# Where the tokens of a feed-forward layer are normalised: in place behind the third pair of products, instead of all at the seventh pair

## The chip, the core and the metric

The kernel runs on one core of a Trainium2 chip. A core has engines that work side by side, each through its own queue of instructions in order: TensorE (PE in the profile, with its weight loads as PEld) for matrix products, VectorE (DVE), ScalarE (ACT) and GpSimd (POOL) for work element by element, and SyncE (SP), which here only issues transfers. Products land in PSUM, eight banks of 128 x 512 floats; everything else lies in SBUF. The metric is the time of one execution on the device in microseconds (us), median over runs.

## The reference

Two layers of an encoder over 512 tokens of width 1024, all in float32. Each layer is an attention block of two kinds of heads, a cross-attention over 256 memory tokens, and a feed-forward block; then a last norm. The change lies in the feed-forward block:

```python
def rms_norm(x, g):
    x32 = x.astype(jnp.float32)
    y = x32 * lax.rsqrt(jnp.mean(x32 * x32, axis=-1, keepdims=True) + EPS)
    return (y * g.astype(jnp.float32)).astype(x.dtype)

def conv_ffn(h, w_up, conv_w, conv_b, w_down):
    u = h @ w_up
    up = jnp.pad(u, ((0, 0), (1, 1), (0, 0)))
    u = up[:, :-2] * conv_w[0] + up[:, 1:-1] * conv_w[1] + up[:, 2:] * conv_w[2] + conv_b
    gate, val = jnp.split(u, 2, axis=-1)
    return (jax.nn.silu(gate) * val) @ w_down

x = x + conv_ffn(rms_norm(x, norm_ffn[l]), w_up[l], conv_w[l], conv_b[l], w_down[l])
```

`w_up` has 2 x 2816 columns: 22 groups of 128 for the gate and 22 for the values.

## The kernel before

**Layout and precision.** Activations lie transposed: features on the 128 partitions, the 512 tokens along the free dimension, so x is eight chunks `xT[c]` of 128 x 512. A float32 product is made of three products of rounded parts: each operand is split into `hi` (a cast, on ACT) and `lo` (the operand less `hi`, a subtraction on DVE or POOL), and `mm3` adds hi·hi, hi·lo and lo·hi in one bank. Weights come by a transfer into one of three `raw` buffers, and are split into one of four `hi`/`lo` pairs, `hi` on ACT and `lo` mostly on POOL (`emit_split`, L740 and L741).

**Operands of the feed-forward block.** The class `Norm` makes, while the memory attention closes, the operands `ffn.ops[c] = (ffn.hi[:, c], ffn.lo[:, c])`: x times the gain of the norm, not yet times the factor 1/rms of each token. That factor is known only when all eight chunks are squared and summed. `ffn.stat()` and `ffn.spread()` then put it over all partitions, as `ffn.psum` in a PSUM bank and `ffn.rep` in SBUF.

**Pairs.** A pair j is 128 gate columns and the 128 value columns beside them, j = 0 to 21. Pairs 0 to 5 are plain: `up_project` makes 24 products of 128 x 512 for each side in a bank of the kind "mm" (there are four), `up_finish` multiplies both banks by `ffn.rep` on DVE (L1809), and `convolve` does the width-3 convolution with one ACT instruction (L1819) and four DVE instructions (L1826) a side, then SiLU (L1828), the product of both sides (L1829) and the hi/lo split of the result `acts[j]` (L1030, L1031). `up_first` does pairs 0 and 1, whose products begin before the factor is known.

Pairs from 6 (`PLAIN`) on go through `up_forms`: a Winograd-like scheme with seven half-size products in place of eight, on sums and differences of weights and of tokens. It needs tokens that carry the factor already: the normalised operands themselves for three of the products, under the names "b11", "b21" and "b22", and four sums t1 to t4 of quarters of the tokens (`token_forms`, split into hi and lo too). In `up_forms` the last product, t4 with "val", adds to a bank in which DVE must first have finished L1903.

**The tokens for the forms, before.** `token_forms` is a generator, moved on at pairs 2 to 5: it scales the eight chunks into four float32 tiles `xn` (L1846, four chunks at pair 2 and four at pair 3), then makes t1 and t3; at pair 6 it is run to its end, and `split_tokens` rewrites `ffn.hi` and `ffn.lo` in place from `xn`: four casts (L1870) and four subtractions (L1871), two of 128 x 512 and two of 128 x 1024, only the halves that the forms use. The rewriting must wait until pair 5 has read the old operands.

**What sets the order.** The program is traced once, then the class `Order` arranges the instructions of PE, ACT, DVE and POOL with a list scheduler of its own: it replays the program with a cost for each instruction, gives each a due time, tries 30 rounds, and keeps the best. The order of each engine is then fixed. So a change in one place can shift instructions elsewhere. It models that DVE and POOL instructions which read SBUF twice share a path. SP's transfers keep the order in which they are written. `sequence()` gives the outer order: pairs 0 to 5, then two rows of the first down projection, then pairs 6 on with rows of the down projection between them.

Of the kernel before, what the change touches and what calls it, by code (L numbers as in the profile page):

```python
# [20 lines left out]
S = 512  # L21
# [5 lines left out]
KC = D // P  # L27
# [8 lines left out]


PLAIN = 6
FIRST_ROWS = 2
HALF = S // 2  # L40
EPS = 1e-6
# [612 lines left out]
def encoder_kernel(ctx: ExitStack, tc: tile.TileContext, t: dict, out: bass.AP):  # L654
# [5 lines left out]
    ACT, DVE, POOL = Free(nc.scalar), Free(nc.vector), Free(nc.gpsimd)  # L660
# [11 lines left out]
    def nm(s):  # L672
        uid[0] += 1
        return f"{s}_{uid[0]}"

    def rtile(shape, dt=F32R):
        return rpool.tile([P, *shape], dt, tag="r", name=nm("r"), padded_shape=[P, *pad(shape)])
# [24 lines left out]
    f = lambda ap: ap.bitcast(F32)  # L702
# [43 lines left out]
    def split_form(src, n, act, eng):  # L746
        hi = wpool.tile([P, 2 * n, P], F32R, tag="hi", name=nm("hi"), padded_shape=[P, KC, P])
        lo = wpool.tile([P, 2 * n, P], F32R, tag="lo", name=nm("lo"), padded_shape=[P, KC, P])
        act.copy(hi, src)  # L749
        eng.tensor_sub(lo, src, f(hi))  # L750
        return hi, lo

    def form_gate(raw, act):
        sums["gate"] = raw
        return split_form(raw, 4, act, POOL)
# [35 lines left out]
    def get_w(key, ahead=AHEAD):  # L791
        n = done[0]
        assert plan[n][0] == key, (plan[n][0], key)
        prepare_w(1 + ahead)
        done[0] += 1
        w = ready[n]
        ready[n] = None
        return w

    def cols(key, w, k0, nk, c0, ncol, eng="P"):  # L800
        src = w[k0 * P : (k0 + nk) * P, c0 : c0 + ncol].rearrange("(k p) c -> p k c", p=P)
        plan.append((key, [(lambda r: r, src)], nk, ncol, eng))

    def plan_up(l, j):
        if j >= PLAIN:
            cols(("gate", j), t["w_up"][l], 0, KC, P * j, P)
            cols(("sums", j), t["w_up"][l], 0, KC, D_FF + P * j, P)
            plan.append((("diffs", j), [], KC, P, "P"))
            plan.append((("val", j), [], KC, P, "P"))
            return  # L810
        cols(("up", j, 0), t["w_up"][l], 0, KC, P * j, P)
        cols(("up", j, 1), t["w_up"][l], 0, KC, D_FF + P * j, P)

    def sequence():


        for g, (j0, nj) in enumerate(GROUPS):
            at = FIRST_ROWS if g == 1 else 0
            if at:
                yield "down", 0, range(at)  # L820
            for i in range(nj):
                yield "up", j0 + i, None
                if g > 0:
                    to = at + (KC - at) * (i + 1) // nj if g == 1 else KC * (i + 1) // nj
                    yield "down", g - 1, range(row, to) if i else range(at, to)
                    row = to
# [67 lines left out]
    def gemm_T(ps, w, ops, ks, first, last, c=slice(0, P)):  # L894
        wh, wl = w
        for k in ks:
            mm3(ps, wh[:, k, c], wl[:, k, c], *ops[k], k == first, k == last)
# [229 lines left out]
    for n in FIRST:  # L1127
# [7 lines left out]
        k = slice(k0, k1)  # L1135
# [13 lines left out]
    for l in range(DEPTH):  # L1149
# [625 lines left out]
        ffn = nn  # L1775
        acts = {}

        def up_project(j, side):
            pm = ps_mm()
            gemm_T(pm, get_w(("up", j, side)), ffn.ops, range(KC), 0, KC - 1)  # L1780
            return pm

        def up_first():


            ws, us = [], []
            for side in range(2):
                ws.append(get_w(("up", 0, side)))
                us.append(ps_mm())
                gemm_T(us[side], ws[side], ffn.ops, range(KC - 1), 0, KC - 1)  # L1790
            for side in range(2):
                gemm_T(us[side], ws[side], ffn.ops, [KC - 1], 0, KC - 1)
                if side == 0:
                    ffn.stat()
            us1 = [up_project(1, 0)]
            ffn.spread()
            up_finish(0, us)
            us1.append(up_project(1, 1))
            up_finish(1, us1)

        def up(j):
            if j >= PLAIN:
                up_forms(j)
                return
            up_finish(j, [up_project(j, side) for side in range(2)])

        def up_finish(j, us):
            for u in us:
                DVE.tensor_mul(u, u, ffn.rep)  # L1809
            convolve(j, us)  # L1810
# [22 lines left out]
        halves = [slice(0, HALF), slice(HALF, S)]  # L1833
        xform = {}

        xn = []

        def quarter(k, n):
            return [xn[2 * k + i][:, :, halves[n]] for i in range(2)]

        def token_forms():


            xn.extend(rtile((2, S), F32) for _ in range(4))
            for c in range(KC):
                DVE.scalar_tensor_tensor(xn[c // 2][:, c % 2], xT[c], ffn.gain(c), ffn.psum, op0=ALU.mult, op1=ALU.mult)  # L1846
                if c == 3:
                    yield
            yield
            made = {}  # L1850
            for name, a, b in (("t1", (0, 1), (0, 0)), ("t3", (1, 1), (0, 1)), ("t2", (1, 1), "t1"), ("t4", (1, 0), "t2")):
                src = made[name] = rtile((4, HALF), F32)
                for i in range(2):
                    k = slice(2 * i, 2 * i + 2)
                    other = made[b][:, k] if isinstance(b, str) else quarter(*b)[i]
                    (POOL if name == "t3" else DVE).tensor_sub(made[name][:, k], quarter(*a)[i], other)  # L1856
                xform[name] = hi, lo = [rtile((4, HALF)) for _ in range(2)]
                ACT.copy(hi, src)
                (POOL if name in ("t2", "t3") else DVE).tensor_sub(lo, src, f(hi))
                yield  # L1860

        def split_tokens():


            for name, k, n in (("b11", 0, 0), ("b21", 1, 0), ("b22", 1, 1)):
                xform[name] = [v[:, 4 * k : 4 * k + 4, halves[n]] for v in (ffn.hi, ffn.lo)]
            for c, n in ((0, HALF), (2, HALF), (4, S), (6, S)):
                hi, lo = (v[:, c : c + 2, :n] for v in (ffn.hi, ffn.lo))
                src = xn[c // 2][:, :, :n]
                ACT.copy(hi, src)  # L1870
                DVE.tensor_sub(lo, src, f(hi))  # L1871

        def up_forms(j):


            a, b, c = ps_s(), ps_t(), ps_mm()
            first, second = (v[:, halves[0]] for v in (a, c))
            ws = {}

            def product(ps, name, part, form, start=True):  # L1880
                if name not in ws:
                    ws[name] = get_w((name, j))
                wh, wl = ws[name]
                hi, lo = xform[form]
                for k in range(4):
                    i = 4 * part + k
                    mm3(ps, wh[:, i], wl[:, i], hi[:, k], lo[:, k], start and k == 0, k == 3, skip_group_check=not start)

            p1, u2 = (lambda v: [v[:, i] for i in range(2)])(tmp((2, HALF)))
            p5 = tmp((HALF,))  # L1890
            low = b[:, halves[0]]
            product(first, "gate", 0, "b11")
            ACT.copy(p1, first)
            product(low, "gate", 1, "b21")
            DVE.tensor_add(low, low, p1)
            product(second, "sums", 0, "t1")
            ACT.copy(p5, second)  # L1897
            product(first, "sums", 1, "t2", False)
            ACT.copy(u2, first)
            product(second, "diffs", 0, "b22", False)  # L1900
            DVE.tensor_add(b[:, halves[1]], second, u2)
            product(first, "diffs", 1, "t3", False)
            DVE.tensor_add(a[:, halves[1]], first, p5)  # L1903
            product(first, "val", 0, "t4", False)
            convolve(j, [b, a])
# [26 lines left out]
        def down_last():  # L1932
# [44 lines left out]
            finish(norms[1], ys[1], True)  # L1977

        forms = token_forms()
        for what, n, rows in sequence():  # L1980
            if what == "down":
                down(n, rows)
            elif n == 0:
                up_first()
            elif n > 1:
                if n < PLAIN:
                    next(forms, None)
                elif n == PLAIN:
                    for _ in forms:
                        pass  # L1990
                    split_tokens()
                up(n)
        if l + 1 < DEPTH:
            nn = Norm(G_MIX, l + 1)
            down_closing(len(GROUPS) - 1)
        else:
            down_last()
# [85 lines left out]
```

## Time and profile before

| | |
|---|---|
| median of 3 runs | 1324.18 us (1322.28 to 1324.24) |
| profiled execution | 1324.98 us |
| its span, first to last instruction | 1323.2 us |
| mean granted TensorE clock | 0.996 |
| PE busy in the span | 1306.0 us |
| DVE, ACT, POOL busy | 1004.2, 783.4, 724.9 us |
| feed-forward of layer 0, first plain pair to the first by forms | about 306 to 382 us |
| the same of layer 1 | about 956 to 1030 us |

A row of the timeline has the start in us, the time in us, the engine, the line, the operation, output<-input by the names of the program without their numbers, the shape and the number of instructions merged; in brackets the idle time of the engine before it and what ended it. Tiles named xg are the operands of a norm, r are general SBUF tiles, t are temporaries, mm, sc and tr are PSUM banks, sf are sums of weights. A row of the windows has for a stretch its length and, for each engine, the busy time and the number of instructions, then the granted clock and the share and rate of DMA. A row of the waits has the total, the number and the longest. Instructions of one engine can overlap by some 0.1 us at their ends, so what one costs in a row of them is the distance of starts.

### The profile page before, as it was taken

Reading aid. Unit: us, or ns where it says so; the run is one execution under the profiler, and the core shown is the slowest. Engines: PE = TensorE matmul, PEld = TensorE weight load, DVE = VectorE, ACT = ScalarE, POOL = GpSimd, SP = SyncE. Lnnn points to the kernel's source line nnn. Section 1 sums busy time; section 2 is a strip of 40 time slices with the busy share of each in tenths; the row PEclk is TensorE's granted clock in tenths of the full one; section 3 lists DMA queues with packets and bytes.
Section 4 is the critical chain, followed back from the end, with each engine's and each line's share of the span. In section 5 each row is a group of like instructions: output and inputs, shape, how many; then the busy total and the mean of one; then the engine's idle time right before and its main releaser. Section 6 shows DMA issues by size and latency. Waiting matters only on the chain.

```text
span 1323.2 us, 21017 instructions
## 1 busy us (share of the span) xinstructions
PE 1306.0 (99%) x7632; PEld 1150.3 (87%) x7632; DVE 1004.2 (76%) x1862; ACT 783.4 (59%) x1450; POOL 724.9 (55%) x520
## 2 busy tenths in 40 slices
PE   9999999999999999999999999999999899999998
PEld 8888888888879999999888888888888899999987
DVE  7569877665998987788545698786758998877874
ACT  6768776565555555555536688765645455555544
POOL 3657965717464544454646579655454544444443
PEclk9999999999999999999999999999999999999999
DMA  8734222313213333333455533232232233333332
GB/s 245 188 120 133 97 79 65 99 44 112 88 50 97 106 112 103 99 101 93 137 156 165 150 90 96 56 89 80 64 90 74 69 108 104 101 97 93 116 98 76
DMA packets 205000, 136.98 MB, mean 104 GB/s; under 512 B 5600, under 2 KB 195040, under 8 KB 204896
## 3 DMA queue, kind: packets, MB, share of 16 engines
q1 hardware_dynamic: 204080, 134.98, 34.7%
q8 instruction: 60, 0.98, 0.3%
q10 hardware_dynamic: 816, 0.66, 0.2%
q14 instruction: 44, 0.36, 0.1%
HBM read 125.65 MB, written 2.10 MB: 97 GB/s over the span
## 4 chain that ended last, share of the span: by engine, by line
PE 91%; DVE 5%; ACT 2%; DMA 1%; issue 1%; POOL 0%; POOLq 0%; SPq 0%; ACTq 0%; DVEq 0%
PE mm L101 62%; PE sc L101 21%; PE tr L101 4%; PE tr L1533 2%; DVE xg L1871 1%; PE tr L1378 1%; DVE r L1856 1%; DMA r<-in_bias 1%; DVE r L1031 1%; PE tr L1720 1%; DMA raw<-in_w_in 0%; ACT t L1356 0%; DVE r L1248 0%; DVE sc L1350 0%; ACT r L1227 0%
## 5 line engine op out<-in xcount | busy, mean ns | idle before, releaser
L741 POOL TENSOR_TENSOR lo<-raw,hi 128x512 fp32r<-128x512 f32 (+3 forms) x230 | 371.3, 1629 | 291.2 <-ACT hi L740 243.5
L101 PE MATMUL mm<-r,hi 128*128 128x512 f32 (+1 forms) x1392 | 398.8, 367 | 0.0
L101 PEld LDWEIGHTS mm<-r,hi 128*128 128x128 f32 x1392 | 245.7, 190 | 34.9
L101 PE MATMUL mm<-xg,hi 128*128 128x512 f32 (+1 forms) x960 | 266.5, 363 | 0.5 <-ACT t L1897 0.3
L101 PE MATMUL mm<-r,lo 128*128 128x512 f32 (+1 forms) x728 | 257.9, 356 | 0.0
L740 ACT CAST hi<-raw 128x512 fp32r<-128x512 f32 (+3 forms) x234 | 167.9, 739 | 130.0 <-PE mm L101 52.3
L101 PEld LDWEIGHTS mm<-xg,hi 128*128 128x128 f32 x960 | 170.5, 189 | 27.3 <-issue 1.0
L101 PE MATMUL mm<-xg,lo 128*128 128x512 f32 (+1 forms) x480 | 173.5, 361 | 0.0
L101 PE MATMUL sc<-r,hi 128*128 128x256 f32 (+1 forms) x832 | 165.9, 294 | 5.7 <-DVE sc L1903 5.0
L750 POOL TENSOR_TENSOR lo<-sf,hi 128x1024 fp32r<-128x1024 f32 x32 | 79.1, 2473 | 140.2 <-ACT hi L749 117.0
L101 PEld LDWEIGHTS mm<-r,lo 128*128 128x128 f32 x728 | 137.9, 189 | 19.8
L101 PEld LDWEIGHTS sc<-r,hi 128*128 128x128 f32 x832 | 135.6, 193 | 12.2 <-issue 3.1
L101 PE MATMUL sc<-r,lo 128*128 128x256 f32 (+1 forms) x416 | 122.0, 293 | 0.0
L101 PE MATMUL mm<-hi,xg 128*128 128x512 f32 (+1 forms) x384 | 111.5, 360 | 2.6 <-DVE r L1231 1.3
L749 ACT CAST hi<-sf 128x1024 fp32r<-128x1024 f32 x64 | 67.1, 1050 | 78.8 <-DVE sf L762 46.3
L750 POOL TENSOR_TENSOR lo<-raw,hi 128x1024 fp32r<-128x1024 f32 x32 | 78.1, 2439 | 47.9 <-ACT hi L749 32.9
L101 PEld LDWEIGHTS mm<-xg,lo 128*128 128x128 f32 x480 | 90.6, 189 | 14.2 <-POOL lo L750 0.2
L1037 POOL TENSOR_SCALAR t<-t,s 128x512 f32<-128x512 f32 (+1 forms) x112 | 66.4, 607 | 52.6 <-DVE s L1517 27.7
L101 PEld LDWEIGHTS sc<-r,lo 128*128 128x128 f32 x416 | 80.4, 193 | 1.3
L101 PEld LDWEIGHTS mm<-hi,xg 128*128 128x128 f32 x384 | 68.1, 189 | 11.8 <-DVE r L1231 1.5
L101 PE MATMUL sc<-r,r 128*128 128x256 f32 (+1 forms) x352 | 74.6, 331 | 0.0
L101 PE MATMUL mm<-lo,xg 128*128 128x512 f32 (+1 forms) x192 | 68.5, 357 | 0.0
(200 smaller groups left out, 2615.5 us busy)
## 6 DMA issues: line engine op xcount, KB each, us to landing
raw<-in_w_up SPq DMA_DIRECT2D x88, 512.0 KB, 3.7
raw<-in_w_down SPq DMA_DIRECT2D x36, 384.0 KB, 3.3
raw<-in_w_in SPq DMA_DIRECT2D x25, 512.0 KB, 4.5
raw<-in_w_mem_kv SPq DMA_DIRECT2D x16, 512.0 KB, 4.2
raw<-in_w_down SPq DMA_DIRECT2D x24, 320.0 KB, 3.1
r<-in_bias SPq DMA_DIRECT2D x16, 384.0 KB, 4.8
r<-r SPq DMA_DIRECT2D x22, 256.0 KB, 3.5
raw<-in_w_in SPq DMA_DIRECT2D x18, 256.0 KB, 4.6
```

The costliest lines, as they stand in the source:

```text
L101: return self.engine.matmul(out, lhsT, rhs, **k)
L740: act.copy(hi[:, k], raw[:, k])
L741: (POOL if eng[0] == "P" else DVE).tensor_sub(lo[:, k], raw[:, k], f(hi)[:, k])
L749: act.copy(hi, src)
L750: eng.tensor_sub(lo, src, f(hi))
L1031: DVE.tensor_sub(lo, ps, f(hi))
L1037: eng.tensor_scalar(e, e, sums[:, col : col + 1], 1.0, op0=ALU.mult, op1=ALU.mult)
L1378: PE.transpose(tr[:, (2 * i + c) * P : (2 * i + c + 1) * P], es[j][:, i, c * P : (c + 1) * P], ident)
L1533: PE.transpose(tr[:, k * P : (k + 1) * P], es[j][:, k * P : (k + 1) * P], ident)
L1720: PE.transpose(tr[:, (2 * c + i) * P : (2 * c + i + 1) * P], e[:, i, c * P : (c + 1) * P], ident)
L1856: (POOL if name == "t3" else DVE).tensor_sub(made[name][:, k], quarter(*a)[i], other)
L1871: DVE.tensor_sub(lo, src, f(hi))
```

## The change

The eight chunks are scaled right behind `up_first`, and `split_tokens` moves from pair 6 to pair 3 (`SCALED`): all eight chunks are cast and subtracted in full, 128 x 512 each, in place, behind the reads of pair 2. From pair 3 on the plain products carry the factor, so pairs 3 to 5 go to `convolve` without the multiplication by `ffn.rep`. The sums t1 to t4 are made one at a time, t1 before pair 3 and the next ones after pairs 3, 4 and 5, in the order t1, t2, t3, t4. `split_form` gets a loop over `CUTS` pieces, which is 1.

```diff
+SCALED = 3
+CUTS = 1
...
-        eng.tensor_sub(lo, src, f(hi))
+        for i in range(CUTS if eng is POOL else 1):
+            c = slice(2 * n * i // CUTS, 2 * n * (i + 1) // CUTS) if eng is POOL else slice(0, 2 * n)
+            eng.tensor_sub(lo[:, c], src[:, c], f(hi)[:, c])
...
-            up_finish(j, [up_project(j, side) for side in range(2)])
+            (up_finish if j < SCALED else convolve)(j, [up_project(j, side) for side in range(2)])
...
-        def token_forms():
+        def scale_tokens():
             xn.extend(rtile((2, S), F32) for _ in range(4))
             for c in range(KC):
                 DVE.scalar_tensor_tensor(xn[c // 2][:, c % 2], xT[c], ffn.gain(c), ffn.psum, op0=ALU.mult, op1=ALU.mult)
-                if c == 3:
-                    yield
-            yield
+
+        def split_tokens():
+            for c in range(KC):
+                hi, lo = ffn.ops[c]
+                src = xn[c // 2][:, c % 2]
+                ACT.copy(hi, src)
+                DVE.tensor_sub(lo, src, f(hi))
+            for name, k, n in (("b11", 0, 0), ("b21", 1, 0), ("b22", 1, 1)):
+                xform[name] = [v[:, 4 * k : 4 * k + 4, halves[n]] for v in (ffn.hi, ffn.lo)]
+
+        def token_forms():
             made = {}
-            for name, a, b in (("t1", (0, 1), (0, 0)), ("t3", (1, 1), (0, 1)), ("t2", (1, 1), "t1"), ("t4", (1, 0), "t2")):
+            for name, a, b in (("t1", (0, 1), (0, 0)), ("t2", (1, 1), "t1"), ("t3", (1, 1), (0, 1)), ("t4", (1, 0), "t2")):
...
-        def split_tokens():
-            for name, k, n in (("b11", 0, 0), ("b21", 1, 0), ("b22", 1, 1)):
-                xform[name] = [v[:, 4 * k : 4 * k + 4, halves[n]] for v in (ffn.hi, ffn.lo)]
-            for c, n in ((0, HALF), (2, HALF), (4, S), (6, S)):
-                hi, lo = (v[:, c : c + 2, :n] for v in (ffn.hi, ffn.lo))
-                src = xn[c // 2][:, :, :n]
-                ACT.copy(hi, src)
-                DVE.tensor_sub(lo, src, f(hi))
...
             elif n == 0:
                 up_first()
+                scale_tokens()
             elif n > 1:
-                if n < PLAIN:
-                    next(forms, None)
+                if n == SCALED:
+                    split_tokens()
+                    next(forms)
                 elif n == PLAIN:
                     for _ in forms:
                         pass
-                    split_tokens()
                 up(n)
+                if SCALED <= n < PLAIN:
+                    next(forms, None)
```

## The prediction

> **What bounds the kernel now.** I read the page first, then the waits of PE, then its timeline where the longest wait stands.
>
> ```profile
> span 1323.2 us, 21017 instructions
> PE 1306.0 (99%) x7632; PEld 1150.3 (87%) x7632; DVE 1004.2 (76%) x1862; ACT 783.4 (59%) x1450; POOL 724.9 (55%) x520
> ...
> PE sc L101 <- DVE sc L1903: 5.0, 2, 2.7
> ```
>
> PE is the bound: work taken from another engine pays only where PE waits for it. PE's longest wait falls twice, once in each layer, at the first pair done by forms (j=6): its last product accumulates in the bank that DVE's add on L1903 must finish first. The timeline of PE shows both places and the pace around them.
>
> ```profile
> 391.14 0.40 PE L101 MATMUL sc<-r,hi 128*128 128x256 f32 x2
> 391.38 0.28 PE L101 MATMUL sc<-r,lo 128*128 128x256 f32 x1
> 393.99 0.35 PE L101 MATMUL sc<-r,hi 128*128 128x256 f32 x1 [2.33 <-DVE sc L1903]
> ...
> 1034.41 0.29 PE L101 MATMUL sc<-r,hi 128*128 128x256 f32 x1
> 1035.04 0.39 PE L101 MATMUL mm<-xg,hi 128*128 128x256 f32 x1 [0.34 <-ACT t L1897]
> 1035.91 0.39 PE L101 MATMUL sc<-r,hi 128*128 128x256 f32 x1 [0.49 <-POOL r L1859]
> ...
> 1043.95 0.39 PE L101 MATMUL mm<-r,hi 128*128 128x512 f32 x1
> 1047.04 0.47 PE L101 MATMUL sc<-r,hi 128*128 128x256 f32 x2 [2.69 <-DVE sc L1903]
> ```
>
> A product of 256 columns starts 0.12 us after the one before it (two from 391.14 to 391.38), one of 512 after 0.23 (three in 0.68, rows further down). So the starts 391.38 to 393.99 lose 2.5 us, 1043.95 to 1047.04 lose 2.9, and the two short gaps from 1034.41 to 1035.91 lose 1.5 less two paces, 1.3. After each long gap the windows show the clock:
>
> ```profile
> core 0: us, PE busy (x) PEld busy (x) DVE busy (x) ACT busy (x) POOL busy (x), PEclk, DMA share, GB/s
> 330.00:384.00 54.00, 54.00 (x248) 45.06 (x248) 49.17 (x83) 30.31 (x41) 25.30 (x12) 1.00 0.24 71
> 384.00:391.00 7.00, 6.86 (x52) 6.32 (x51) 7.00 (x3) 1.85 (x4) 7.00 (x3) 1.00 0.01 2
> 395.60:399.10 3.50, 3.50 (x15) 3.17 (x15) 2.91 (x6) 0.78 (x1) 1.61 (x1) 0.51 0.57 169
> 1047.60:1051.00 3.40, 3.40 (x15) 3.01 (x14) 2.23 (x5) 1.74 (x3) 0.00 (x0) 0.50 0.58 171
> ```
>
> For 3.4 us the granted clock is half, which costs another 1.7 us a layer. In 330 to 384, the pairs before, PE is never idle: there is nothing to win there, only to lose.
>
> Why DVE is late stands in the chain of waits, then in its timeline beside POOL's:
>
> ```profile
> 382.76 6.68 DVE xg L1871 x2
> ...
> 377.77 1.45 DVE L1871 TENSOR_TENSOR xg<-r,xg 128x512 fp32r<-128x512 f32 x1
> 379.74 1.28 DVE L1856 TENSOR_TENSOR r<-r,r 128x512 f32<-128x512 f32 x2
> 382.08 7.37 DVE L1871 TENSOR_TENSOR xg<-r,xg 128x512 fp32r<-128x512 f32 x3
> ...
> 1021.88 1.30 DVE L1871 TENSOR_TENSOR xg<-r,xg 128x512 fp32r<-128x512 f32 x1
> 1031.81 5.13 DVE L1871 TENSOR_TENSOR xg<-r,xg 128x512 fp32r<-128x512 f32 x3
> ...
> 382.19 2.83 POOL L1859 TENSOR_TENSOR r<-r,r 128x1024 fp32r<-128x1024 f32 x1 [3.52 <-ACT r L1858]
> 384.98 3.38 POOL L750 TENSOR_TENSOR lo<-sf,hi 128x1024 fp32r<-128x1024 f32 x1
> 388.32 2.83 POOL L741 TENSOR_TENSOR lo<-raw,hi 128x768 fp32r<-128x768 f32 x1
> ```
>
> The four L1871 are the in-place splits that the change moves: 8.8 us of DVE in layer 0 (1.45 + 7.37), 6.4 in layer 1, while three POOL instructions in a row run beside them.
>
> **The change part by part.** *The seventh pair.* DVE loses there the four splits and the two t2 subtractions (1.28): 10.1 us in layer 0, 7.7 in layer 1, against waits of 2.5 and 2.9. The add on L1903 is then held by its own input, no longer by DVE's queue. Removed: 2.5 + 1.7 in layer 0, 2.9 + 1.7 + 1.3 in layer 1, 10.1 us. I leave 0.3 a layer for short waits of the kind at 1034.41, which have ACT and POOL behind them: bounds 0 and 1.3.
>
> *The multiplication by rep* falls away for j=3 to 5, six a layer of 0.69 us (342.82 below), all under busy PE: worth nothing by itself, but it is the room for the rest. The CUTS loop runs once and changes nothing. The swap of t2 and t3, and t1 to t4 one pair each earlier than their use, lie under PE at 100%: nothing, and if that cover were gone their price is that of any DVE wait at j=6. SP's transfers are the same ones in the same order.
>
> *The transition to j=3* is the new danger: eight chunks of the operands must be scaled, cast and subtracted in place while j=2 still reads them. The rows of before that give place and price:
>
> ```profile
> 329.83 0.70 PE L101 MATMUL mm<-xg,hi 128*128 128x512 f32 x2
> ...
> 340.16 0.61 PE L101 MATMUL mm<-xg,hi 128*128 128x512 f32 x2
> 340.84 0.61 PE L101 MATMUL mm<-xg,hi 128*128 128x512 f32 x2
> ...
> 326.47 3.22 DVE L1826 SCALAR_TENSOR_TENSOR t<-mm,par,t 128x504 f32<-128x504 f32 x8 [0.25 <-ACT t L1819]
> ...
> 337.43 0.69 DVE L1829 TENSOR_TENSOR mm<-mm,t 128x512 f32<-128x512 f32 x1
> 338.03 0.74 DVE L1846 SCALAR_TENSOR_TENSOR r<-xT,par,tr 128x512 f32<-128x512 f32 x1
> 338.68 0.74 DVE L1826 SCALAR_TENSOR_TENSOR t<-mm,par,t 128x504 f32<-128x504 f32 x1
> ...
> 342.82 0.69 DVE L1809 TENSOR_TENSOR mm<-mm,rep 128x512 f32<-128x512 f32 x1
> ...
> 338.38 0.57 ACT L1030 CAST r<-mm 128x512 fp32r<-128x512 f32 x1
> ...
> 337.88 2.40 POOL L741 TENSOR_TENSOR lo<-raw,hi 128x1024 fp32r<-128x1024 f32 x1 [3.55 <-ACT hi L740]
> 343.34 2.40 POOL L741 TENSOR_TENSOR lo<-raw,hi 128x1024 fp32r<-128x1024 f32 x1 [3.06 <-ACT hi L740]
> ```
>
> The 48 products of j=2 start at 329.83, those of j=3 at 340.84, three products in 0.68 us (340.16 to 340.84). The order of each engine is fixed when the program is built; up to 337.43 it is that of before, and then DVE has
>
> ```
> scale 0, 1, 2; split of acts j=1; split 0, scale 3, split 1, scale 4, split 2, scale 5,
> split 3, scale 6, split 4, scale 7, split 5, 6, 7; rep-multiply of j=2; eight conv steps of j=2
> ```
>
> A scale takes 0.65 us of DVE (338.03 to 338.68), a subtraction 0.60 (337.43 to 338.03). Three scales end at 339.98, the acts split at 340.58, split 0 with its 0.68 at 341.3; then one chunk each 1.25 us: 342.5, 343.8, 345.0, 346.3, 347.5, and 348.1, 348.7 for the last two. ACT's cast of a chunk (0.57) follows its scale and is ready in time: the first starts at 338.95. PE's order alternates j=3's two sides, so a chunk feeds six products, 1.36 us, more than the 1.25 it takes to come. PE waits 0.25 for chunk 0 (its second product could start at 341.07) and 0.35 for chunk 1, then no more: 0.6 us. The two halves of the cover are that POOL is quiet (its split at 337.88 ends at 340.28, and the next weight cast stands behind the eight casts on ACT, so that POOL's at 343.34 moves to about 348.7), and that the weights it then splits are wanted only by j=4's second side, at 340.84 + 10.9 + 5.4 = 357.
>
> Queued behind the eight splits is j=2's own convolution, which frees a PSUM bank for j=4: 348.65 + 0.6 + 3.2 = 352.45, where PE comes at 340.84 + 10.9 + 0.6 = 352.3. That is 0.2 us more. Where a product waits is fixed by these rows within bounds of 0 (ACT and DVE gain a little) and one POOL split, 2.4.
>
> The rows on the lock between DVE and POOL:
>
> ```profile
> 358.73 1.85 POOL L741 TENSOR_TENSOR lo<-raw,hi 128x768 fp32r<-128x768 f32 x1 [2.19 <-ACT hi L740]
> ...
> 359.63 2.03 DVE L1859 TENSOR_TENSOR r<-r,r 128x1024 fp32r<-128x1024 f32 x1
> 393.76 1.21 DVE L1859 TENSOR_TENSOR r<-r,r 128x1024 fp32r<-128x1024 f32 x1
> ```
>
> The same instruction takes 1.21 alone and 2.03 when POOL is on until 360.58: it waits until POOL ends. The Trainium skill, "SBUF — State Buffer", section "Who interferes with whom", says just that of a DVE instruction with two SBUF inputs, and that whichever comes second is blocked whole; the trace agrees, and the rule speaks against this change, whose eight splits all have two SBUF inputs. By it each POOL instruction that starts among them costs up to its own length; the forecast holds none there, the third and fourth rivals do.
>
> **The sum.** −10.1 + 2 × (0.6 + 0.2 + 0.3) = −7.9 us. The profiled run took 1324.98, its span 1323.2 and 1.8 around it; it stands 0.8 above the median, so the sum, made on its span, goes over to the median: 1324.2 − 7.9 = 1316.3.
>
> **The rivals.** *The seventh pair stays late in one layer*: behind DVE come ACT and POOL, which split j=6's weights late (POOL is on without a break from 384 to 391). Then 2.9 + 1.7 stay: 1316.3 + 4.6 = 1320.9. For it speak the waits on ACT and POOL at 1035; against it that POOL's t2 and t3 work also moves ahead of this stretch. 17%.
>
> *One collision at j=3 in each layer*: a POOL weight split among the eight, 2.4 us, and the half clock after it, 1.7: 1316.3 + 8.2 = 1324.5, no change. Against it stands the order above. The Trainium skill, "TensorE: Matmul & The Clock Gate", section "What's actually happening", has the half rate come after an idle window of about 3.4 us; here gaps of 2.6 sufficed, so by the page the clock term would be nothing and the time 1316.3 + 4.8 = 1321.1. 10%.
>
> *Slower*: DVE and POOL take turns through the whole transition, as they did at j=6, where three splits took 7.37 us instead of 0.60 + 1.13 + 1.13 (the second and third are twice as long): 2.6 times. Eight splits would take 12.4 us for 4.8, so 7.6 more and 1.7 of half clock in each layer: 1316.3 + 18.6 = 1334.9. It decides from 4.2 us a layer on. For it speaks that it is the same line of work; against it that POOL has one weight split in 5.5 us here (337.88, 343.34), and three in a row there. 9%.
>
> **How the numbers follow.** The forecast has 64%, with its own range from 1312.3 (all 10.1 gone at no cost, 1314.1, and an estimated 1.8 either way because the order is built anew for the whole program) to 1319 (1.3 left at j=6 in both layers, a part of a collision at j=3). The whole range reaches to the first rival: 1312.3 to 1321.2. About 0.2%, 2.6 us, can be told from no change. Faster: 64 + 17 = 81%; within: 10%; slower: 9%.
>
> **What would show it.** PE's wait on the add of the seventh pair is gone from its list, and with it both half-clock windows. DVE's splits of a chunk, now after j=2, take 0.68 each, and PE's waits for them add to about 0.6 a layer; a POOL split among them, or splits of 2 us, shows the third and fourth cases. If the j=4 products wait for a bank by more than 0.5, the convolution was put too far back. Wrong would also be a gain that comes from stretches before 330 us.

## The result, and the profile after

| | before | after |
|---|---|---|
| median, 13 runs each in turn | 1323.31 us (1321.88 to 1326.2) | 1320.61 us (1316.09 to 1321.8) |
| ratio, 95% interval | | 0.9972 [0.9962, 0.9982] |
| profiled execution | 1324.98 us | 1318.48 us |
| its span | 1323.2 us | 1316.7 us |

The change is faster by 2.7 us in the median, inside the whole range and 4.3 us above the forecast. It lies above the forecast's own range, which ended at 1319; the whole range takes it in only because it reaches to the first rival. The profiled execution gained more, 6.5 us. On two other chips, where both kernels ran again, the changed one had 1317.17 against 1324.18 us (ratio 0.9949 [0.9936, 0.9961]) and 1317.82 against 1323.88 (0.9953 [0.9941, 0.9966]), 6 to 7 us.

Lines are numbered anew: L101 is now L103, L741 is L743, L750 is L754, L1809 is L1813, L1846 is L1850, L1856 is L1872, the POOL line L1859 is L1875, L1002 is L1006, and L1903 is L1908. The in-place split, L1871 before, is **L1859** now. First the page of the changed kernel, and its list of PE's waits (total, times, longest).

```profile
span 1316.7 us, 21053 instructions
PE 1303.8 (99%) x7632; PEld 1146.9 (87%) x7632; DVE 1003.9 (76%) x1858; ACT 786.6 (60%) x1458; POOL 721.2 (55%) x520
```

```profile
PE tr L103 <- POOL ident masks.py:199: 1.3, 1, 1.3
PE tr L103 <- DVE t L1006: 1.3, 1, 1.3
...
PE mm L103 <- DVE xg L1859: 0.3, 1, 0.3
...
PE mm L103 <- DVE t L1830: 0.2, 1, 0.2
```

The wait on the add of the seventh pair, 5.0 us and the longest before, isn't in the list. New are two short ones of the transition (L1859, L1830) and one of 1.3 on L1006, which has nothing to do with the feed-forward block. The windows over the seventh pair of both layers (columns as in the prediction's windows) show a PE that is busy all through, at the full clock:

```profile
384.00:391.00 7.00, 7.00 (x60) 7.00 (x59) 4.86 (x6) 3.54 (x6) 4.56 (x3) 1.00 0.45 131
391.00:402.00 11.00, 11.00 (x78) 10.25 (x77) 11.00 (x18) 5.45 (x8) 5.06 (x3) 1.00 0.22 64
...
1033.00:1043.00 10.00, 10.00 (x77) 9.62 (x77) 9.05 (x12) 4.68 (x7) 5.68 (x3) 1.00 0.33 95
1043.00:1056.00 13.00, 13.00 (x93) 12.23 (x92) 11.98 (x18) 7.43 (x12) 6.67 (x3) 1.00 0.38 112
```

DVE has 4.86 us of work in 384 to 391, where it had 7.00, and POOL 4.56 of 7.00. At the transition to j=3, PE's timeline shows the price:

```profile
340.01 0.39 PE L103 MATMUL mm<-xg,lo 128*128 128x512 f32 x1
340.24 1.01 PE L103 MATMUL mm<-xg,hi 128*128 128x512 f32 x2
341.09 0.39 PE L103 MATMUL mm<-xg,lo 128*128 128x512 f32 x1
341.32 1.20 PE L103 MATMUL mm<-xg,hi 128*128 128x512 f32 x3
342.35 0.40 PE L103 MATMUL mm<-xg,lo 128*128 128x512 f32 x1
...
351.71 0.39 PE L103 MATMUL mm<-xg,lo 128*128 128x512 f32 x1
352.21 0.70 PE L103 MATMUL mm<-xg,hi 128*128 128x512 f32 x2
```

Three starts from 340.01 to 341.09 should take 0.68 and take 1.08; four from 341.09 to 342.35 should take 0.91 and take 1.26. So 0.40 and 0.35 go to waiting for chunks 0 and 1, and 0.27 (0.50 less one pace) to the bank for j=4. DVE and POOL at that place:

```profile
340.02 0.68 DVE L1859 TENSOR_TENSOR xg<-r,xg 128x512 fp32r<-128x512 f32 x1
340.62 0.74 DVE L1850 SCALAR_TENSOR_TENSOR r<-xT,par,tr 128x512 f32<-128x512 f32 x1
341.27 0.69 DVE L1859 TENSOR_TENSOR xg<-r,xg 128x512 fp32r<-128x512 f32 x1
...
346.31 1.89 DVE L1859 TENSOR_TENSOR xg<-r,xg 128x512 fp32r<-128x512 f32 x3
...
337.30 2.42 POOL L743 TENSOR_TENSOR lo<-raw,hi 128x1024 fp32r<-128x1024 f32 x1 [3.54 <-ACT hi L742]
348.14 4.89 POOL L743 TENSOR_TENSOR lo<-raw,hi 128x1024 fp32r<-128x1024 f32 x2 [8.43 <-ACT hi L742]
```

A chunk takes 1.25 us (340.02 to 341.27), and POOL is silent from 339.72 to 348.14, behind the casts on ACT.

For the whole span I add up what each product starts later than the pace of its shape after the one before it. Waits and half clock are both in this **loss of PE**, in us:

| stretch | before | after |
|---|---|---|
| transition to j=3, 329 to 378 and 974 to 1026 | 0.39 + 0.39 | 1.30 + 1.78 |
| seventh pair, 378 to 402 and 1026 to 1053 | 5.21 + 5.87 | 0.03 + 0.03 |
| everything else | 16.62 | 18.84 |
| sum | 28.48 | 21.98 |

The seventh pair gave 11.0, the transitions took 2.3 and the rest 2.2: 6.5 us, the difference of the spans. One gap of 0.26 at the start of j=2 is in both kernels, but at 328.76 after it lies just ahead of the first stretch and counts in the rest; counted alike, the transitions took 2.6 and the rest 1.9. Of that rest, the largest item is the wait on L1006. There DVE adds the squares of the last chunk for the first norm of layer 1. In the timelines of DVE and POOL, after, then before:

```profile
658.76 3.72 DVE L1006 TENSOR_TENSOR t<-t,t 128x512 f32<-128x512 f32 x1
...
656.88 5.05 POOL L743 TENSOR_TENSOR lo<-raw,hi 128x512 fp32r<-128x512 f32 x4
```

```profile
663.80 1.51 DVE L1002 TENSOR_TENSOR t<-t,t 128x512 f32<-128x512 f32 x1
...
660.94 6.76 POOL L741 TENSOR_TENSOR lo<-raw,hi 128x512 fp32r<-128x512 f32 x5
```

The same add with two SBUF inputs falls into a run of POOL's weight splits both times. Before, it came through in 1.51 us; after, it ended at 662.48, 0.55 us behind the fourth split (661.93). Nothing in the diff touches this place; the order of the engines was built anew.

### The profile page after: what moved, and what is told of

It reads as the page before. It is cut to its first block, busy times and chain, and to the rows that moved or that the text cites. A ratio compares the mean times of both kernels' runs of the same rounds, so it can differ in the third digit from the quotient of the medians.

```text
span 1316.7 us, 21053 instructions
## 1 busy us (share of the span) xinstructions
PE 1303.8 (99%) x7632; PEld 1146.9 (87%) x7632; DVE 1003.9 (76%) x1858; ACT 786.6 (60%) x1458; POOL 721.2 (55%) x520
## 4 chain that ended last, share of the span: by engine, by line
PE 89%; DVE 6%; ACT 2%; issue 1%; DMA 1%; POOL 0%; SPq 0%; POOLq 0%; DVEq 0%; ACTq 0%
PE mm L103 61%; PE sc L103 20%; PE tr L103 4%; PE tr L1537 2%; DVE t L1830 1%; DMA xT<-in_xT 1%; DVE t L1006 1%; PE tr L1382 1%; DVE r L1850 1%; PE tr L1724 1%; DVE r L1035 1%; DVE xg L1859 0%; DVE r L1252 0%; ACT t L1360 0%; ACT r L1034 0%
## 5 line engine op out<-in xcount | busy, mean ns | idle before, releaser
L743 POOL TENSOR_TENSOR lo<-raw,hi 128x512 fp32r<-128x512 f32 (+3 forms) x230 | 370.5, 1624 | 288.5 <-ACT hi L742 238.2
L103 PE MATMUL mm<-r,hi 128*128 128x512 f32 (+1 forms) x1392 | 396.5, 366 | 0.0
L103 PEld LDWEIGHTS mm<-r,hi 128*128 128x128 f32 x1392 | 245.3, 189 | 34.8
L103 PE MATMUL mm<-xg,hi 128*128 128x512 f32 (+1 forms) x960 | 267.3, 363 | 1.1 <-DVE xg L1859 0.3
L103 PE MATMUL mm<-r,lo 128*128 128x512 f32 (+1 forms) x728 | 257.5, 356 | 0.0
L103 PEld LDWEIGHTS mm<-xg,hi 128*128 128x128 f32 x960 | 170.1, 189 | 30.2 <-DVE xg L1859 2.7
L103 PE MATMUL mm<-xg,lo 128*128 128x512 f32 (+1 forms) x480 | 173.5, 361 | 0.0
L103 PE MATMUL sc<-r,hi 128*128 128x256 f32 (+1 forms) x832 | 162.6, 291 | 0.0
L754 POOL TENSOR_TENSOR lo<-sf,hi 128x1024 fp32r<-128x1024 f32 x32 | 77.6, 2426 | 148.3 <-ACT hi L751 112.1
L103 PEld LDWEIGHTS mm<-r,lo 128*128 128x128 f32 x728 | 137.5, 189 | 19.8
L103 PEld LDWEIGHTS sc<-r,hi 128*128 128x128 f32 x832 | 133.8, 191 | 4.9
L103 PE MATMUL sc<-r,lo 128*128 128x256 f32 (+1 forms) x416 | 121.1, 291 | 0.0
L103 PE MATMUL mm<-hi,xg 128*128 128x512 f32 (+1 forms) x384 | 111.3, 360 | 1.3 <-DVE r L1252 1.3
L103 PEld LDWEIGHTS mm<-xg,lo 128*128 128x128 f32 x480 | 90.7, 189 | 13.8
L754 POOL TENSOR_TENSOR lo<-raw,hi 128x1024 fp32r<-128x1024 f32 x32 | 77.5, 2422 | 44.5 <-PE mm L103 25.0
L103 PEld LDWEIGHTS sc<-r,lo 128*128 128x128 f32 x416 | 79.6, 191 | 1.2
L103 PEld LDWEIGHTS mm<-hi,xg 128*128 128x128 f32 x384 | 68.0, 190 | 10.5 <-DVE r L1252 1.5
L103 PE MATMUL sc<-r,r 128*128 128x256 f32 (+1 forms) x352 | 74.3, 330 | 0.0
L765 DVE TENSOR_TENSOR sf<-raw 128x512 f32<-128x512 f32 x32 | 62.7, 1960 | 8.2 <-DMA raw<-in_w_up 8.2
```

The source lines that it names most:

```text
L103: return self.engine.matmul(out, lhsT, rhs, **k)
L743: (POOL if eng[0] == "P" else DVE).tensor_sub(lo[:, k], raw[:, k], f(hi)[:, k])
L754: eng.tensor_sub(lo[:, c], src[:, c], f(hi)[:, c])
L765: DVE.tensor_add(both[:, :4], raw[:, :4], raw[:, 4:])
```

## Experiments

The prediction gave one cause for the late add, the in-place splits in DVE's queue; the expectations of the halves call this theory A. The rival, called C there and B in the last run, is that the token sums t2 and t4 were late by their own way (subtractions on DVE, cast on ACT, split on POOL or DVE), and that the splits matter less. In the other expectations the letters stand for other questions, which each text states. Ratios are to the kernel before, on the same chip. "Loss" is that of the table above: the two transitions, the two seventh pairs. The gap of 0.26 lies ahead of the first stretch in the rows "after again", "scaled from pair 4", "multiplication kept" and the last one, so their first number is that much too low beside the others.

| run | median us (range, runs) | ratio, 95% | loss at transitions | at seventh pairs |
|---|---|---|---|---|
| before again | 1324.43 (1322.29–1325.69, 11) | 0.9999 [0.999, 1.0008] | 0.36 + 0.40 | 5.24 + 5.69 |
| after again | 1317.17 (1317.01–1317.49, 5) | 0.9949 [0.9936, 0.9961] | 1.30 + 1.77 | 0.03 + 0.06 |
| before, other order | 1323.36 (1321.74–1325.09, 11) | 0.9994 [0.9985, 1.0003] | 0.53 + 0.43 | 3.66 + 3.01 |
| after, other order | 1316.71 (1315.81–1319.88, 5) | 0.995 [0.9937, 0.9962] | 1.58 + 1.57 | 0.03 + 0.06 |
| sums early only | 1317.57 (1314.53–1324.86, 10) | 0.9953 [0.9936, 0.997] | 0.37 + 0.35 | 0.49 + 1.91 |
| splits early only | 1323.52 (1319.37–1328.82, 10) | 0.9996 [0.9977, 1.0014] | 1.57 + 1.75 | 1.91 + 1.18 |
| scaled from pair 4 | 1316.46 (1315.28–1318.46, 4) | 0.9935 [0.9918, 0.9952] | 0.10 + 0.38 | 0.89 + 0.16 |
| multiplication kept | 1324.44 (1323.23–1334.17, 10) | 1.0012 [0.9991, 1.0032] | 2.61 + 2.62 | 2.29 + 0.04 |
| after, third time | 1317.82 (1316.58–1318.68, 5) | 0.9953 [0.9941, 0.9966] | 1.57 + 1.77 | 0.03 + 0.03 |
| after, PE sums the square | 1318.00 (1317.72–1318.49, 5) | 0.9956 [0.9943, 0.9968] | 1.58 + 1.75 | 0.03 + 0.03 |
| from pair 4, PE sums the square | 1317.32 (1316.97–1318.64, 5) | 0.995 [0.9937, 0.9964] | 0.50 + 0.36 | 0.89 + 0.89 |
| sums early only, PE sums the square | 1316.13 (1314.70–1317.38, 5) | 0.9942 [0.993, 0.9955] | 0.01 + 0.37 | 0.49 + 0.56 |

**Both kernels again, and both with another order.** The first two are unchanged. In the next two only the seed of the search for the order differs.

```diff
-... SEED = 30, 4, 100.0, (0.0, 0.0, 0.5, 1.0, 2.0), 500, 4
+... SEED = 30, 4, 100.0, (0.0, 0.0, 0.5, 1.0, 2.0), 500, 5
```

> The kernel before, run again, for a second trace and the clock of each run. Theory A (the change wins about 8 us in its two stretches every time, and the median shows less because waits and half-clock windows elsewhere come and go): the wait before the last product of the seventh pair and the half clock behind it stand in both layers again, 10 to 11 us of PE time over the pace in those two stretches; the rest of the program differs from the first trace by under 2 us. Theory B (the stretch itself varies from run to run, and the first trace of before was a bad draw): the loss at the seventh pair is 4 to 8 us here, and a layer without a half-clock window is found.

> The changed kernel run again. Theory A: from the third pair to the eighth the loss over the pace of PE is 1.2 to 1.5 us a layer as in the first trace, and what makes a run slower than 1318 lies elsewhere: a half-clock window of 3.4 us (1.7 us lost) behind a wait outside these stretches, most likely behind the wait of 1.3 us for the sum of squares at the start of layer 1. Theory B: in a slow run a half-clock window or a wait of over 1 us stands within the two stretches.

> The kernel before with another seed for the scheduler's draws: the same instructions in another order. Theory A: the order built anew moves the time by 1 to 3 us either way without any change of work, and most of it at the seventh pair or in the attention of layer 1. Theory B: under 1 us either way.

> The changed kernel with that other seed. Theory A: in the two stretches the loss is again 1 to 2 us a layer; the total lies 1 to 3 us from the changed kernel, by waits elsewhere. Theory B: total within 1 us of the changed kernel.

The second traces show the same as the first: the seventh pairs lose 10.9 us before and 0.1 after. At the places of the change the two differ by 8.5 us, and everywhere else by 0.4 (16.2 against 15.8).

With the other order the change is worth 1323.36 − 1316.71 = 6.6 us, with its own on the same chip 7.0. So the gain isn't an accident of one order. What another order moves is 0.5 to 1.1 us, less than the 1.8 that the prediction put on it. The order that the third kernel got makes the seventh pair cheaper (6.7 against 10.9 us of loss) without being much faster.

**One half of the change at a time.** In the first kernel the chunks are scaled and the sums made as in the change, but the splits stand at the seventh pair, in the form of before, and the multiplication by `ffn.rep` stays. In the second the splits are early and the multiplication is gone, but the sums are made as before. Both scale the chunks early, as the change does; that alone was not run.

```diff
 sums early only
-            (up_finish if j < SCALED else convolve)(j, [up_project(j, side) for side in range(2)])
+            up_finish(j, [up_project(j, side) for side in range(2)])
...
                 if n == SCALED:
-                    split_tokens()
                     next(forms)
                 elif n == PLAIN:
                     for _ in forms:
                         pass
+                    split_tokens()
```

```diff
 splits early only
...
-                if n == SCALED:
+                if n < SCALED:
+                    pass
+                elif n == SCALED:
                     split_tokens()
+                elif n < PLAIN:
                     next(forms)
                 elif n == PLAIN:
...
-                if SCALED <= n < PLAIN:
-                    next(forms, None)
```

> One part alone: the chunks are scaled behind the first pairs and the sums t1 to t4 made around pairs j=3 to 5 as in the changed kernel, but the splits in place stay at j=6 and the multiplication by rep stays for j=3 to 5. Theory A (DVE's queue at j=6 is late by the four splits, 8.8 and 6.4 us, more than by the sums): the wait before the last product of j=6 stays in part, 1 to 3 us a layer with its half clock; time 1319 to 1323. Theory C (it is the sums t2 and t4 with POOL's splits beside them that make DVE late): the wait is gone, no loss at j=3 either, time 1314 to 1317, better than the changed kernel.

> The other part alone: splits in place behind j=2 and no multiplication for j=3 to 5, as in the changed kernel, but the sums are made at the places of before, t1 ahead of j=4, t3 ahead of j=5, t2 and t4 at j=6. Theory A: the wait at j=6 is gone all the same, because 10 us of DVE work have left; loss at j=3 as in the changed kernel; time within 1 us of the changed kernel. Theory C: the wait at j=6 stays, 1 to 3 us a layer; time 1320 to 1324.

The sums alone bring the ratio of the whole change, 0.9953 against 0.9949 to 0.9953. Their median, 1317.57, lies just above the 1314 to 1317 of theory C and below the 1319 of theory A, and one wait is left that C did not expect. The splits alone bring nothing that the median shows, 0.9996, as C expected (1320 to 1324). The timelines say why. Sums early only, DVE, POOL and PE:

```profile
379.54 2.95 DVE L1859 TENSOR_TENSOR xg<-r,xg 128x512 fp32r<-128x512 f32 x3
...
384.15 1.28 DVE L1872 TENSOR_TENSOR r<-r,r 128x512 f32<-128x512 f32 x2
...
1029.33 3.50 DVE L1872 TENSOR_TENSOR r<-r,r 128x512 f32<-128x512 f32 x2
...
1035.61 2.84 DVE L1875 TENSOR_TENSOR r<-r,r 128x1024 fp32r<-128x1024 f32 x1
...
385.39 2.40 POOL L754 TENSOR_TENSOR lo<-sf,hi 128x1024 fp32r<-128x1024 f32 x1 [6.93 <-ACT hi L751]
...
1038.93 0.48 PE L103 MATMUL sc<-r,hi 128*128 128x256 f32 x2 [1.64 <-DVE sc L1908]
```

The three splits that took 7.37 us before take 2.95 at the same place: with t2 and t3 made earlier, they come 2.5 us sooner, and POOL is idle until 385.39. In layer 0 all four splits stand ahead of the add and it comes in time, so their number in DVE's queue wasn't by itself what made it late. In layer 1 POOL still falls on t4 (3.50 and 2.84 us), and 1.64 of waiting stays.

Splits early only:

```profile
384.03 5.20 DVE L1872 TENSOR_TENSOR r<-r,r 128x512 f32<-128x512 f32 x2
...
391.74 3.34 DVE L1875 TENSOR_TENSOR r<-r,r 128x1024 fp32r<-128x1024 f32 x1
...
383.46 2.41 POOL L1875 TENSOR_TENSOR r<-r,r 128x1024 fp32r<-128x1024 f32 x1 [6.56 <-PE mm L103]
385.83 2.85 POOL L754 TENSOR_TENSOR lo<-sf,hi 128x1024 fp32r<-128x1024 f32 x1
388.64 2.29 POOL L743 TENSOR_TENSOR lo<-raw,hi 128x768 fp32r<-128x768 f32 x1
391.61 2.39 POOL L754 TENSOR_TENSOR lo<-raw,hi 128x1024 fp32r<-128x1024 f32 x1 [0.67 <-ACT hi L751]
...
395.48 0.50 PE L103 MATMUL sc<-r,hi 128*128 128x256 f32 x2 [1.63 <-DVE sc L1908]
```

Here the splits are gone from DVE's queue, and t4 is stuck all the same: its two subtractions take 5.20 us (1.28 when POOL is quiet), its `lo` 3.34 (1.21), beside four POOL instructions. Before, t4's subtractions were stuck too, behind the splits:

```profile
389.37 2.94 DVE L1856 TENSOR_TENSOR r<-r,r 128x512 f32<-128x512 f32 x2
```

The trace does show a gain at the seventh pair, 11.1 to 3.1 us, so theory A isn't without substance: either half alone takes most of that loss away (the sums 11.1 to 2.4). But 2.5 us of it go to the transitions. The 5.5 that are left at these places don't show in the median, which is 0.8 us under that of the kernel before, within the interval. The ten runs scatter from 1319.37 to 1328.82; the profiled one, 1321.0, is among the shorter. Which wait the longer ones have, no trace shows.

**One pair later, and the multiplication kept.** In the first kernel `SCALED` is 4. In the second the plain pairs from j=3 multiply by a tile of ones where the multiplication by `ffn.rep` stood.

```diff
-SCALED = 3
+SCALED = 4
```

```diff
+            if SCALED <= j < PLAIN:
+                for u in us:
+                    DVE.tensor_mul(u, u, onesrep)
```

> The changed kernel with the splits one pair later, behind j=3. The loss at the transition (0.25 + 0.35 for the first two chunks, 0.3 to 0.4 for the PSUM bank of the next pair but one) should vanish in part, since the scaling is done by then and a chunk costs DVE only 0.6: 0 to 0.5 us a layer in place of 1.2 to 1.5. Theory A: no wait at j=6, time 1 to 2 us under the changed kernel. Rival: DVE has one pair less for the sums, a wait at j=6 of 1 us or more comes back, time 1 to 4 us over it.

> The changed kernel with the six multiplications a layer put back, by a tile of ones, at j=3 to 5: 6 x 0.6 = 3.6 us of DVE. Theory A (they are the room for the rest: DVE is 99% busy from 345 to 384 in the changed kernel): DVE comes late at j=6 again or frees the PSUM banks late, 1 to 4 us a layer lost, time 1318 to 1325. Rival (the removal is worth nothing): time within 0.7 us of the changed kernel.

One pair later loses 0.10 + 0.38 at its transition, 2.6 us less than the change, and 0.89 + 0.16 at the seventh pair, 1.0 more. By its ratio the time is that of the change within the intervals. Beside each other on one chip, both with the later edit of the square, the two (1317.32 and 1318.00 us) differ by 0.7 us, and by 0.75 in loss at these places. With the multiplication back, the whole gain is lost. Its trace:

```profile
344.48 2.26 DVE L1864 TENSOR_TENSOR xg<-r,xg 128x512 fp32r<-128x512 f32 x1
...
346.79 0.50 PE L103 MATMUL mm<-xg,hi 128*128 128x512 f32 x1 [1.20 <-DVE xg L1864]
...
395.22 0.50 PE L103 MATMUL sc<-r,hi 128*128 128x256 f32 x2 [1.98 <-DVE sc L1913]
```

One split of the transition meets POOL (2.26 us for 0.68), PE waits 1.20 for it, and the seventh pair is late again by 1.98. At these places the trace loses 4.4 us more than the change. Not all of the lost gain is there: another 3.2 us go at the start of layer 1 (650 to 671), on a wait and a stretch at half clock that the next section looks at, where the change's traces lose 1.7 or 0.1. Sums early only kept the real multiplication and lost nothing at the transitions: in these runs the room is needed only by a kernel that also splits behind pair 2.

**The wait at the start of layer 1.** The trace of the version from pair 4 has the wait on L1006 too, with a stretch at half clock behind it, in PE's timeline and the windows:

```profile
662.03 1.05 PE L103 MATMUL tr<-ones,t 128*128 128x1 f32 x8 [1.29 <-DVE t L1006]
```

```profile
664.20:667.60 3.40, 3.40 (x10) 2.64 (x9) 0.00 (x0) 0.00 (x0) 0.56 (x1) 0.50 0.71 206
```

Wait and half clock together are 3.3 us of loss there (650 to 671), against 1.7 after and 0.1 before. Did this make the changed kernel 3 us slower on the first chip than on the two others? The last four kernels ran together on one chip: the change unchanged, and three in which PE sums the last chunk's square by itself, so that the add on L1006 falls away.

```diff
+            self.extra = []
...
+            elif c == KC - 1 and self.gcol == G_MIX and self.l > 0:
+                self.extra.append(sq)
...
-                self.rstd, self.var = rsqrt(sums(self.acc), nb, 1.0 / D, factor)
+                self.rstd, self.var = rsqrt(sums(self.acc, *self.extra), nb, 1.0 / D, factor)
```

> The changed kernel once more, as the yardstick for the three beside it on this chip. All theories: 1316 to 1321 us, ratio to the kernel before 0.994 to 0.998. Theory L (the spread between the changed kernel's runs comes from the start of layer 1, where VectorE's last accumulation of a norm's squares is stuck behind PoolE's back-to-back splits: 1.45 us of TensorE waiting, and some 1.7 us more in the runs in which a stretch at half clock follows): its runs fall into groups about 3 us apart. Rival S (the spread is of the chip, anywhere in the span): no such groups.

> The changed kernel with one edit in layer 1's norm in front of the feed-forward-like mixer part: the last chunk's square is not accumulated by VectorE but summed by TensorE with four more one-column products, about 0.4 us. Theory L: the idle stretch of TensorE near 660 us (1.45 us) is under 0.4 us in the trace, no stretch at half clock stands between 655 and 670 us, and the median is 1 to 3 us under that of the changed kernel beside it, its runs within 1315 to 1318 us. Rival S: the wait goes to another operand of the same norm, the median is within 0.5 us of the changed kernel's and the spread of its runs stays.

> The same edit in the version that scales the chunks from the fifth pair (one pair later than the change), so that the transition to the fourth pair costs 0.1 to 0.4 us a layer instead of 1.2 to 1.4. Theory L: 1314 to 1316 us, the fastest of the four. Rival S: as the changed kernel, 1316 to 1319 us.

> The sums and the scaling early, the splits in their old place at the seventh pair, with the same edit at the start of layer 1. Theory B (the token sums' way through VectorE, ScalarE and PoolE is all that was late; where the splits stand is worth under 1 us): within 1 us of the changed kernel with the same edit. Theory A (the splits in VectorE's queue at the seventh pair are what is late): 4 us or more over it.

Theory L isn't borne out. The change's five runs lie within 2.1 us, in no groups, and its trace has no wait on L1006 here at all; taking the add away left the median where it was (1318.00 against 1317.82). The timelines of the third run of the change and of the edit show its price:

```profile
662.28 0.95 PE L103 MATMUL tr<-ones,t 128*128 128x1 f32 x8
663.09 0.72 PE L103 MATMUL sc<-xg,hi 128*128 128x512 f32 x2
```

```profile
662.22 1.84 PE L103 MATMUL tr<-ones,t 128*128 128x1 f32 x16
663.92 0.72 PE L103 MATMUL sc<-xg,hi 128*128 128x512 f32 x2
```

There are eight products of one column more, not four, and they cost 1.70 − 0.81 = 0.9 us in every run, where I had put 0.4. What does vary from run to run of the same program stands in the waits of that third run:

```profile
PE mm L103 <- DVE r L1235: 1.4, 1, 1.4
```

This wait, in layer 0 near 74 us, is not in the change's first list above 0.2 and is 0.7 long in its second trace. So the "everything else" of one profile is good to some 1.5 us only. Why the first chip gave 1320.61 is left open.

The last kernel decides between the halves: with the same edit on the same chip, leaving the splits in their old place is faster than moving them, 1316.13 against 1318.00 us, each of its five runs under each of the other's. That is 1.9 us, more than the 1 us of theory B: by the traces it saves 2.6 us at the transitions, counted alike, and loses 1.0 more at the seventh pair. It beats the kernel before by 7.8 us.

## Why the prediction was right, and where its reasons were not

**Bound.** Right: PE is at 99% in both, and the loss of PE accounts for the whole difference of the spans.

**Seventh pair.** The size held: 10.1 less 0.6 was predicted to go, 11.0 went, with both stretches at half clock. Short waits for which 0.3 a layer was left aren't there.

**Its cause** is the step that failed. The prediction read the 8.8 us of the four splits beside three POOL instructions, put the late add on DVE's queue, that is on the splits and the two subtractions of t2, and priced "t1 to t4 one pair each earlier than their use" at nothing. The runs show that the lateness came from two streams that met, and that moving either one takes most of it away: 11.1 to 2.4 us with the sums early, 11.1 to 3.1 with the splits early. The part that was priced at nothing earns in the median what the whole change earns. The splits alone pay 2.5 us at the transitions and earn nothing that the median shows. A row that hints at it is in the prediction: POOL's L1859 at 382.19, the `lo` of t2, is the first of the three that ran beside those 7.37 us.

**Transition.** Forecast 0.6 for two chunks and 0.2 for a bank; measured 0.75 and 0.27 in layer 0. In layer 1 the same row for a chunk (988.58 to 989.30) loses 0.49 and that for the bank (1000.15 to 1000.76) 0.38. The rhythm of 1.25 us a chunk and POOL's return at 348.14 (forecast about 348.7) came as worked out from the fixed order and the durations. The Trainium skill, "SBUF — State Buffer", section "Who interferes with whom", spoke against the change here; none of the eight splits of either layer collided in the change's traces (0.68 to 0.71 us each), but in the version with the multiplication kept one did, 2.26 us for 0.68.

**Multiplication by rep.** "Worth nothing by itself, but it is the room for the rest" held for this change: giving the room back lost the whole gain, 4.4 us of it at the places named.

**Elsewhere.** The estimate of 1.8 either way was exceeded in the profiled run, +2.2 us (1.9 with the gap at the start of j=2 counted alike). That explains its −6.5 against the −7.9 forecast: −8.7 at the places of the change, +2.2 elsewhere. In the second traces it was −8.5 and −0.4, so this part varies from run to run and is not a price of the change.

**Rivals.** The measured 1320.6 is the time of the first rival, 1320.9, but not by its mechanism: the seventh pair is late in neither layer. That the range took in the median of the first chip is luck. On the other two chips the change is at 1317.2 and 1317.8, 0.9 and 1.5 above the forecast.

## What to carry to other kernels

When a stretch of one engine looks slow beside another, ask which of the two streams would be enough to move: the splits here were the victim, and taking the sums out from beside them made them fast in place. When both halves of a change can be run alone, run them alone: here the cheaper half had all the gain, and the dearer half paid for itself at best. An edit that makes room for another has no worth of its own to measure, and is only seen by putting the load back.

## What the runs showed of the hardware

A blocked DVE instruction can stay blocked across several POOL instructions: the add at 658.76 took 3.72 us beside splits of 1.3 us each that followed one another without a gap, and 3.77 with the multiplication kept (at 661.77). The prediction's bound of one POOL instruction for a collision was too low. In the third run of the change the same add came through at the first boundary, in 1.22 us.

The half clock doesn't follow from the length of the gap. It came after idle gaps of 2.33 and 2.69 us in the kernel before (2.31 and 2.72 in its second trace), after one of 1.29 in the version from pair 4 and one of 1.27 at the same place with the multiplication kept. It didn't come after a gap of the same 1.29 in the changed kernel, nor after 1.98 with the multiplication kept, nor with the other order of the kernel before, where the starts at the seventh pair lie 2.60 us apart (2.61 with its own order, which brought it). Each such stretch in the middle of a span lasted 3.4 us. The Trainium skill, "TensorE: Matmul & The Clock Gate", section "What's actually happening", has windows of that length that run freely and one idle window before the half rate; the length agrees, while the longest gap here that brought it was 2.72 us.

Where a gap falls does separate the cases. In the kernel before the stretches at half clock start at 395.65, 1047.60 and 1320.66, which are 191 and 80 times 3.413 us apart. When every trace is cut into windows of 3.413 us laid back from such a start, the window just ahead of a stretch in the middle of the span lacked 2.1 to 2.9 us of products (counting products of one column as idle), and no other window in the middle of the span, in 14 traces, lacked more than 1.9. The gap of the other order lies across the edge of two windows, and the first of them lacks 1.85. This is a count made on traces at hand; no run moved a gap on purpose.
